# One fast-product operand, T4 of X, formed at another place: with the first pair's products instead of with the last gMLP blocks

## The chip, the core and the metric

The kernel runs on one core of a Trainium2 chip. Its engines work side by side and wait for each other through semaphores: TensorE (PE) multiplies into PSUM, VectorE (DVE) and ScalarE (ACT) do elementwise work, GpSimd (POOL) does some elementwise work and starts transfers, SyncE (SP) only starts transfers. Each engine takes its own instructions strictly in their order. The metric is device time in microseconds (us), from runs of the whole program.

## The reference

One layer of a decoder trunk on 1024 tokens of width 1024, in float32. What matters here is the input projection of the normalized tokens, `hn`, and the first mixer, gMLP:

```python
hn = rms_norm(h, norm_mix_g[l])
proj = jnp.einsum('bsd,de->bse', hn, w_in[l])
za, zb, zc, xbc, dt_raw, g_raw = jnp.split(proj, SPLIT_POINTS, axis=-1)
ya = gmlp_mixer(za, ...)    # u * (lower-triangular mix of layer_norm(v) + b), u, v = split(gelu(za))
...
gates = jax.nn.sigmoid(g_raw.reshape(bsz, seq, N_BRANCHES, D_MODEL) + b_gate[l])
merged = (gates[:, :, 0] * jnp.einsum('bse,ed->bsd', ya, w_branch_a[l])
          + gates[:, :, 1] * jnp.einsum('bse,ed->bsd', yb, w_branch_b[l])
          + gates[:, :, 2] * jnp.einsum('bse,ed->bsd', yc, w_branch_c[l]))
```

## The kernel before

**Numbers.** A float32 operand is held as two float32r parts, high and low. `split` (L129 to L133) makes them: ACT casts the high part (L132), then DVE subtracts it from the source for the low part (L133). A product is three matmuls: high by high, high by low, low by high.

**Two ways to multiply.** The columns of `proj` that need work right away are made in units of 128 columns (`product`, L555, PSUM tile `ps`). The gates, z and the Hawk gate come later, in *pairs* of 128-column blocks, by a fast scheme with seven products of half size in place of eight. Its right operands are quarters of the normalized tokens X and sums of them: B11, B21, B22, T1, T2, T3, T4. Each is four tiles of 128 x 512 in two parts. Its left operands are quarters of the pair's weights and sums of them (A.., S1 to S4). `seventh` (L478) issues the 12 matmuls of one of the seven products.

**The seven products of a pair** stand in class `Pair`, in the order in which the loop calls them:

- p1: A11 by B11 into bank b1, copied out by ACT (L983)
- p2: A12 by B21 into a bank of its own, added to p1's copy by DVE (L988)
- p4 of the pair before: A22 by T4 on top of that pair's b1
- p5: S1 by T1 into bank b2, copied out by ACT (L994)
- p6: S2 by T2 on top of b1, copied out by ACT (L1000)
- p3: S4 by B22 on top of b2, added by DVE (L1004)
- p7: S3 by T3 on top of b1, added by DVE (L1008)

A product on top of a bank has to wait until the copy of what the bank held is done: p6 waits for L983, p3 for L994, p7 for L1000. p4 of a pair runs in the next pair, so the first pair's T4 is first read after the second pair's p2.

**The place of the sums of X.** `x_forms` (L856) is a generator that makes T3, T2, T1 and T4, for two pieces kp = 0 and 1 in turn. `later` puts a generator on a list, and `step` advances each on it by one `yield`. The first gMLP unit starts it, and one step follows each later unit. A gMLP unit is `product`, a GELU (L235 to L238: two ACT and two DVE instructions) and, a step later, the mixing: 16 small matmuls (L838), two DVE instructions (L839), and on POOL the product with u (L841) and its store (L842). T3's two parts are written into tiles of X itself (L893 to L895), so this split waits until the last unit has read them. The first pair's weights are loaded and summed by `first_pair` (`cast1`, `sums1`, `sums2` at L502 to L507, `cast12`), also by steps.

**What sets the order.** In the gMLP stage a scheduler orders the instructions of each engine. In the loop over pairs, `with tc.manual_schedule()` keeps them as written: each engine has them in the order of the calls.

```python
z.w.cast22()
while z:
    nxt = Pair(*pairs.pop(0)) if pairs else None
    z.p1()
    z.w.cast34()
    step()
    z.p2()
    ...
        nxt.w.cast1()
    ...
    step()
    z.p5()
```

Of the kernel before, what the change touches and what calls it, by code (L numbers as in the profile page):

```python
# [8 lines left out]
F32 = mybir.dt.float32  # L9
# [27 lines left out]
def trunk_kernel(ctx: ExitStack, tc: tile.TileContext, x, norm_mix_g, w_in, b_gate, gmlp_ln_g, gmlp_ln_b,  # L37
# [30 lines left out]
    def nm(s):  # L68
        uid[0] += 1
        return f"{s}_{uid[0]}"  # L70

    def act(shape=(P, T), dt=F32):
        return pools[0].tile(list(shape), dt, tag="act", name=nm("a"))

    def half_(shape=(P, HF), dt=F32):
        return halfp.tile(list(shape), dt, tag="half", name=nm("h"))
# [51 lines left out]
    def split(dst_hi, dst_lo, src, eng=None, cast=None):  # L128
        if cast:  # L129
            cast.tensor_copy(out=dst_hi, in_=src)  # L130
        else:
            actv(dst_hi, src, AF.Copy)  # L132
        (eng or nc.vector).tensor_tensor(out=dst_lo, in0=src, in1=dst_hi.bitcast(F32), op=ALU.subtract)  # L133
# [62 lines left out]
    X = Pairs(lambda shape, dt_: xp.tile(list(shape), dt_, tag="xn", name=nm("xn")))  # L196
# [334 lines left out]
    queue, ready, pending = [], [], []  # L531
# [4 lines left out]
    def later(gen):  # L536
        pending.append(gen)

    def step():
        for g_ in list(pending):  # L540
            try:
                next(g_)
            except StopIteration:
                pending.remove(g_)
# [281 lines left out]
    def gmlp_unit(g):  # L826
        def stages(u2):
            if g == 0:
                later(x_forms())
            elif g == 5:  # L830
                later(first_pair())
            yield
            vg = v_of.pop(g)
            y = act()
            for half in range(2):
                ps = aux()
                for i in range(4):
                    mm(ps[:, i * P:(i + 1) * P], vg[:, half * 4 + i, :], wT[:, g, :], start=True, stop=True)  # L838
                stt(out=y[:, hsl(half)].rearrange("p (c t) -> p c t", t=P), in0=ps.rearrange("p (c t) -> p c t", t=P),  # L839
                    scalar=vh[:, LNG + g:LNG + g + 1], in1=bs[:, g, :].unsqueeze(1).to_broadcast([P, 4, P]), op0=ALU.mult, op1=ALU.add)  # L840
            nc.gpsimd.tensor_tensor(out=y, in0=y, in1=u2, op=ALU.mult)  # L841
            nc.gpsimd.dma_start(out=yd["a"][g], in_=y)  # L842

        def post(ps):
            u2 = act()
            gelu2(u2, ps, T)
            later(stages(u2))
            v_group(g + 1)

        unit_in(C_U + g * P, post)  # L850
# [2 lines left out]
    XF = {n: [[X.rhs(part, 4 * kh + kk, th) for kk in range(4)] for part in range(2)]  # L853
          for n, kh, th in (("B11", 0, 0), ("B21", 1, 0), ("B22", 1, 1), ("T3", 0, 1))}

    def x_forms():  # L856
        third = []
        for n in ("T1", "T2", "T4"):
            XF[n] = [[None] * 4, [None] * 4]
        for kp in range(2):  # L860
            def quarter(part, kh, th):
                return X.tile(part, th, 2 * kh + kp).bitcast(F32)

            def in_halves(name, t):
                for kk in range(2):
                    pr = half_((P, 4, P), F32R), half_((P, 4, P), F32R)
                    for part in range(2):
                        XF[name][part][2 * kp + kk] = pr[part]
                    split(pr[0], pr[1], t[:, kk])

            third.append(act((P, 2, 4, P)))
            t3, d, e = third[kp], act((P, 2, 4, P)), act((P, 2, 4, P))
            tt(out=t3, in0=quarter(0, 1, 1), in1=quarter(0, 0, 1), op=sub)
            tt(out=e, in0=quarter(1, 1, 1), in1=quarter(1, 0, 1), op=sub)
            tt(out=t3, in0=t3, in1=e, op=ALU.add)
            yield
            tt(out=d, in0=quarter(0, 0, 0), in1=t3, op=ALU.add)
            tt(out=d, in0=quarter(1, 0, 0), in1=d, op=ALU.add)
            in_halves("T2", d)
            yield  # L880
            tt(out=e, in0=quarter(0, 1, 1), in1=d, op=sub)
            tt(out=e, in0=quarter(1, 1, 1), in1=e, op=ALU.add)
            in_halves("T1", e)
            yield
            tt(out=d, in0=quarter(0, 1, 0), in1=d, op=sub)
            tt(out=d, in0=quarter(1, 1, 0), in1=d, op=ALU.add)
            pr = act((P, 2, 4, P), F32R), act((P, 2, 4, P), F32R)
            split(pr[0], pr[1], d)
            for part in range(2):
                for kk in range(2):  # L890
                    XF["T4"][part][2 * kp + kk] = pr[part][:, kk]
            yield
        assert not queue  # L893
        for kp in range(2):
            split(X.tile(0, 1, kp), X.tile(1, 1, kp), third[kp])  # L895

    actx_pool = []
    two = (P, 2, HF)
# [194 lines left out]
    def w_load(b, name, new, key=None):  # L1093
        L[b, key or name] = [new(two) for _ in range(2)]
        for h, t in enumerate(L[b, key or name]):
            nc.sync.dma_start(out=t, in_=w_view(b, name, h))
# [7 lines left out]
    def y_first(b, new):  # L1104
        R[b, "first"] = [new(two, F32R) for _ in range(2)]
        for h, t in enumerate(R[b, "first"]):
            nc.sync.dma_start(out=t.bitcast(F32), in_=y_view(b, "B21", h))
# [10 lines left out]
    def sums_load(b):  # L1118
        w_load(b, "A21", w4, "S")
        for h in range(2):  # L1120
            add_into(L[b, "S"][h], w_view(b, "A22", h))
# [10 lines left out]
    def make(b, i, s):  # L1132

        side, h = (s // 2) ^ (i == 3), s % 2
        new = op_new(b, i, side)
        pr = OP.setdefault((b, i), ([], []))[side]
        if side == 0:
            src = L[b, ("A12", "A11", "S", "A12", "S", "A21", "A22")[i]][h]
            hi, lo = new(two, F32R), new(two, F32R)
            split(hi, lo, src)  # L1140
            if i == 2:
                actv(src, src, AF.Copy, scale=-1.0)
                add_into(src, L[b, "A11"][h])
                for k in range(2 * h):
                    add_into(L[b, "A12"][k], L[b, "S"][k])
            elif i == 4:
                t = L[b, "A21"][h]
                tt(out=t, in0=L[b, "A11"][h], in1=t, op=sub)
        elif i == 0:
            lo = R[b, "first"][h]  # L1150
            hi = new(two, F32R)
            split(hi, lo, lo.bitcast(F32))
        else:
            hi, lo = new(two, F32R), new(two, F32R)
            split(hi, lo, R[b, ("", "B11", "B11", "B22", "B11", "B12", "B21")[i]][h])
            r = lambda name: R[b, name][h]
            if i == 1:
                tt(out=r("B11"), in0=r("B12"), in1=r("B11"), op=sub)
            elif i == 3:
                tt(out=r("B11"), in0=r("B11"), in1=r("B22"), op=sub)  # L1160
                tt(out=r("B12"), in0=r("B22"), in1=r("B12"), op=sub)
            elif i == 4:
                tt(out=r("B21"), in0=r("B21"), in1=r("B11"), op=ALU.add)
        pr.append((hi, lo))
# [113 lines left out]
    gx = ExitStack()  # L1278
    actx_pool.append(gx.enter_context(tc.tile_pool(name="actx", bufs=4, reuse_waits="tile")))
    z, prev = cur.pop(), None  # L1280
    with tc.manual_schedule():
        z.w.cast22()
        while z:
# [5 lines that stand above are left out]
            if prev:  # L1289
                step()  # L1290
                prev.p4()
            if nxt:
                nxt.w.cast1()
            else:
                w_load(0, "A12", r4)
                y_first(0, act)
                w_load(0, "A11", w4)
            step()
            z.p5()
            if nxt:  # L1300
                nxt.w.sums1()
            else:
                make(0, 0, 2)
            step()
            z.p6()
            if nxt:
                nxt.w.sums2()
                nxt.w.cast12()
            else:
                sums_load(0)  # L1310
                make(0, 0, 3)
            step()
            z.p3()
            if nxt:
                nxt.w.cast22()
            else:
                make(0, 0, 0)
            step()
            z.p7()
            if not nxt:  # L1320
                make(0, 0, 1)
            step()
            prev, z = z, nxt
# [532 lines left out]
```

## Time and profile before

| | |
|---|---|
| median of 3 runs | 1964.87 us (1964.46 to 1967.53) |
| the profiled execution's own time | 1964.1 us |
| its span, first to last instruction | 1962.4 us |
| mean granted TensorE clock | 0.991 |
| busy: PE, DVE, ACT, POOL | 97%, 72%, 52%, 13% |
| gMLP units end, first pair begins | 597.8 us, 601.3 us |

PE is busy nearly all the time, so what counts are the few places where it stands still or runs at a lower clock. The change lies between some 540 and 640 us of the span.

### The profile page before, as it was taken

How to read it: one execution, taken by the hardware profiler on the slowest of the kernel's cores; microseconds unless marked ns; L12 is line 12 of the kernel's file. 1: busy time of each engine (PE TensorE's matmuls, PEld its weight loads, DVE VectorE, ACT ScalarE, POOL GpSimd, SP SyncE). 2: the span in 40 equal slices, each digit the busy share in tenths (PEclk: the TensorE clock that was granted, in tenths of full speed). 3: DMA queues.
4: the chain of work that ended last, by engine and by line, in shares of the span. 5: the costliest groups of instructions: out<-in, count | busy, mean ns of one | idle time of the engine just before them, and what ended most of it. 6: DMA issues, size and time to landing. Idle time of an engine off the chain costs nothing.

```text
span 1962.4 us, 23743 instructions
## 1 busy us (share of the span) xinstructions
PE 1905.5 (97%) x8928; PEld 1587.2 (81%) x8928; DVE 1407.0 (72%) x2018; ACT 1014.6 (52%) x1471; POOL 262.5 (13%) x358
## 2 busy tenths in 40 slices
PE   8999999999999999999999999998999999999996
PEld 7998888888887787878778887877788887888885
DVE  5485868787758767677777888248665567787787
ACT  6425859686534545454554544167455555243253
POOL 4111122121342010100010110000211110000000
PEclk9999999999999999999999999999999999999998
DMA  4256575566754343434497987331544448553532
GB/s 162 59 147 140 119 151 122 125 154 138 166 137 153 108 150 108 150 108 129 138 286 263 275 222 199 107 108 54 198 135 170 149 169 298 168 172 118 183 118 86
DMA packets 211015, 301.25 MB, mean 154 GB/s; under 512 B 13028, under 2 KB 125876, under 8 KB 210900
## 3 DMA queue, kind: packets, MB, share of 16 engines
q1 hardware_dynamic: 167348, 158.54, 26.5%
q0 software_dynamic: 34544, 119.69, 22.8%
q10 hardware_dynamic: 9008, 21.51, 3.1%
q8 instruction: 70, 1.15, 0.3%
q14 instruction: 45, 0.37, 0.1%
HBM read 195.75 MB, written 74.58 MB: 138 GB/s over the span
## 4 chain that ended last, share of the span: by engine, by line
PE 82%; DVE 8%; ACT 5%; DMA 3%; issue 2%; POOL 0%; ACTq 0%; SPq 0%; DVEq 0%; POOLq 0%
PE aux L478 40%; PE ps L555 18%; PE gps L478 11%; PE aux L257 4%; PE aux L1378 2%; PE aux L791 1%; DMA c<-yc_d 1%; PE aux L727 1%; PE aux L723 1%; ACT a L1427 1%; PE aux L703 1%; DVE a L133 1%; DVE rsq_q L111 1%; ACT wt L132 1%; DMA a<-g_d 1%
## 5 line engine op out<-in xcount | busy, mean ns | idle before, releaser
L555 PE MATMUL ps<-xn,wh 128*128 128x512 f32 x1088 | 295.0, 392 | 0.0
L478 PE MATMUL aux<-b,b 128*128 128x512 f32 x1152 | 264.4, 389 | 1.0 <-DVE b L133 0.8
L478 PEld LDWEIGHTS aux<-b,b 128*128 128x128 f32 x1152 | 216.0, 188 | 47.0 <-DVE b L133 1.7
L555 PEld LDWEIGHTS ps<-xn,wh 128*128 128x128 f32 x1088 | 202.9, 188 | 42.2 <-issue 0.9
L478 PE MATMUL aux<-a,b 128*128 128x512 f32 x960 | 219.4, 389 | 0.0
L478 PEld LDWEIGHTS aux<-a,b 128*128 128x128 f32 x960 | 180.2, 188 | 37.4
L555 PE MATMUL ps<-xn,wl 128*128 128x512 f32 x544 | 168.3, 389 | 0.0
L478 PE MATMUL gps<-xn,wt 128*128 128x512 f32 x684 | 158.7, 389 | 2.1 <-DVE a L238 2.1
L478 PE MATMUL aux<-b,wt 128*128 128x512 f32 x672 | 156.9, 389 | 0.0
L478 PEld LDWEIGHTS gps<-xn,wt 128*128 128x128 f32 x684 | 128.2, 188 | 29.1 <-issue 2.5
L478 PEld LDWEIGHTS aux<-b,wt 128*128 128x128 f32 x672 | 126.1, 188 | 26.2
L132 ACT ACTIVATE b<-wt 128x1024 fp32r<-128x1024 f32 x88 | 90.7, 1052 | 85.4 <-DMA wt<-u_d 56.0
L133 DVE TENSOR_TENSOR wt<-a,wt 128x1024 fp32r<-128x1024 f32 x66 | 80.9, 1225 | 66.8 <-ACT wt L132 66.8
L555 PEld LDWEIGHTS ps<-xn,wl 128*128 128x128 f32 x544 | 102.1, 188 | 21.5
L133 DVE TENSOR_TENSOR b<-wt,b 128x1024 fp32r<-128x1024 f32 x88 | 107.2, 1219 | 15.5 <-ACT b L132 15.5
L1608 DVE TENSOR_TENSOR a<-aux,a 128x512 f32<-128x512 f32 x112 | 77.0, 689 | 50.4 <-PE aux L478 50.4
L133 DVE TENSOR_TENSOR a<-a,a 128x1024 fp32r<-128x1024 f32 (+1 forms) x68 | 66.6, 986 | 41.0 <-ACT a L132 40.9
L133 DVE TENSOR_TENSOR wt<-rt,wt 128x1024 fp32r<-128x1024 f32 x35 | 42.8, 1224 | 57.1 <-ACT wt L132 57.0
L132 ACT ACTIVATE a<-a 128x1024 fp32r<-128x1024 f32 (+1 forms) x68 | 55.9, 837 | 53.0 <-DVE a L1560 45.3
L478 PE MATMUL aux<-a,wt 128*128 128x512 f32 x336 | 78.7, 390 | 3.4 <-ACT a L1485 3.4
L478 PEld LDWEIGHTS aux<-a,wt 128*128 128x128 f32 x336 | 62.9, 188 | 17.2 <-ACT a L1485 4.2
L132 ACT ACTIVATE wt<-a 128x1024 fp32r<-128x1024 f32 x66 | 69.6, 1055 | 8.7 <-DVE a L506 8.3
(350 smaller groups left out, 3526.5 us busy)
## 6 DMA issues: line engine op xcount, KB each, us to landing
wt<-u_d SPq DMA_DIRECT2D x54, 512.0 KB
u_d<-a POOLq DMA_DIRECT2D x48, 512.0 KB, 5.5
raw<-in_w_in_dram SPq DMA_DIRECT2D x34, 512.0 KB
wl<-raw POOLq DMA_DIRECT2D x34, 512.0 KB, 5.2
g_d<-a POOLq DMA_DIRECT2D x24, 512.0 KB, 3.2
a<-g_d ACTq DMA_DIRECT2D x24, 512.0 KB
rt<-in_w_in_dram SPq DMA_DIRECT2D x19, 512.0 KB
a<-in_w_in_dram SPq DMA_DIRECT2D x19, 512.0 KB
```

The costliest lines, as they stand in the source:

```text
L111: stt(out=q, in0=r, scalar=nh, in1=r, op0=ALU.mult, op1=ALU.mult)
L132: actv(dst_hi, src, AF.Copy)
L133: (eng or nc.vector).tensor_tensor(out=dst_lo, in0=src, in1=dst_hi.bitcast(F32), op=ALU.subtract)
L257: mm(ps[:, :nt], X.tok(a, k, c), wk[k][w], start=(k == 0 and i == 0), stop=(k == KD - 1 and i == 2))
L478: mm(ps, lhs[l][kk], rhs[r][kk], start=(new and n == 0), stop=(n == 11), skip_group_check=not new)
L555: mm(ps[:, hsl(h)], w[wi][:, k, :], a.rhs(ai, k, h), start=(n == 0), stop=(n == 3 * KD - 1))
L703: mm(st[:, cc * 256:cc * 256 + 256], Bt[:, 2 * q + cc, :], xw[q][:, cc].rearrange("p h d -> p (h d)"), start=True, stop=True)
L723: mm(yo[:, tok(i)], pv[c // 2][:, c % 2, j * P:(j + 1) * P], Cf[:, tok(c)], start=True, stop=True)
L727: mm(yi[64 * h:64 * h + 64, tok(i)], xdt[c // 2][:, c % 2, 2 * j + h, :], E[c // 2][:, c % 2, 2 * j + h, :], start=True, stop=True)
L791: mm(ps, w[wi][:, q * P:(q + 1) * P], S["xs"][half][ai], start=(n == 0), stop=(n == 2))
L1378: mm(ps, M.tok(a, k, c), wo[nb][k][w], start=(k == 0 and a + w == 0), stop=(k == KD - 1 and a == 1))
L1608: tt(out=h, in0=ps, in1=h, op=ALU.add)
```

## The change

`x_forms` no longer makes T4. It keeps the tile that holds T2's sum (`d`, in the list `second`), from which T4 is made. A new generator, `x_last`, makes T4 for kp = 0 and then kp = 1. It is put on the list just ahead of the loop over pairs. The first pair's first `step` (behind p1 and `cast34`) so issues T4 for kp = 0, and its second `step` (behind p2 and the next pair's `cast1`) T4 for kp = 1. With one `yield` less per piece, `x_forms` gets to its other sums for kp = 1 one unit earlier, and to the split of T3 two steps earlier: that is still beside the last gMLP units.

```diff
+    third, second = [], []
+
     def x_forms():
-        third = []
         for n in ("T1", "T2", "T4"):
             XF[n] = [[None] * 4, [None] * 4]
         for kp in range(2):
...
             in_halves("T1", e)
             yield
+            second.append(d)
+        assert not queue
+        for kp in range(2):
+            split(X.tile(0, 1, kp), X.tile(1, 1, kp), third[kp])
+
+
+    def x_last():
+        for kp in range(2):
+            def quarter(part, kh, th):
+                return X.tile(part, th, 2 * kh + kp).bitcast(F32)
+
+            d = second[kp]
             tt(out=d, in0=quarter(0, 1, 0), in1=d, op=sub)
             tt(out=d, in0=quarter(1, 1, 0), in1=d, op=ALU.add)
             pr = act((P, 2, 4, P), F32R), act((P, 2, 4, P), F32R)
...
             yield
-        assert not queue
-        for kp in range(2):
-            split(X.tile(0, 1, kp), X.tile(1, 1, kp), third[kp])
...
     z, prev = cur.pop(), None
+    later(x_last())
     with tc.manual_schedule():
         z.w.cast22()
```

Three places show what it does to the order. PE, POOL and SP keep theirs. In the changed file T4's sums are L898 and L899 (before: L885 and L886), and the lines of `Pair` are ten higher (L993, L998 and L1004 are the former L983, L988 and L994).

DVE from the last unit's GELU (L236, L238) to the low part of S1 and S2 (`wt_5437`), before. `a_5234` is T4's sum for kp = 1 (L886 its second instruction), `a_5433` its low part, `h_` the halves of T1, `a_5409` and `a_5410` the weights' sums, `a_5415` a gMLP output:

```order
L236 SCALAR_TENSOR_TENSOR a_5390<-a_5390,ps_5340 128x1024
L133 TENSOR_TENSOR h_5402<-a_5235,h_5401 128x512
L886 TENSOR_TENSOR a_5234<-xn_246,a_5234 128x1024
L238 SCALAR_TENSOR_TENSOR a_5389<-a_5390,ps_5340 128x1024
L502 TENSOR_TENSOR a_5409<-a_5337 128x512
L503 TENSOR_TENSOR a_5410<-rt_5336,a_5337 128x512
L506 TENSOR_TENSOR a_5409<-a_5409,rt_5336 128x512
L839 SCALAR_TENSOR_TENSOR a_5415<-aux_5416,vh,bs 128x512
L507 TENSOR_TENSOR a_5410<-rt_5336,a_5409 128x512
L839 SCALAR_TENSOR_TENSOR a_5415<-aux_5422,vh,bs 128x512
L133 TENSOR_TENSOR a_5433<-a_5234,a_5432 128x1024
L133 TENSOR_TENSOR wt_5437<-a_5409,wt_5436 128x1024
```

The same stretch of DVE in the changed kernel; `wt_5429` is now the low part of S1 and S2:

```order
L236 SCALAR_TENSOR_TENSOR a_5394<-a_5394,ps_5344 128x1024
L238 SCALAR_TENSOR_TENSOR a_5393<-a_5394,ps_5344 128x1024
L502 TENSOR_TENSOR a_5407<-a_5341 128x512
L503 TENSOR_TENSOR a_5408<-rt_5340,a_5341 128x512
L506 TENSOR_TENSOR a_5407<-a_5407,rt_5340 128x512
L839 SCALAR_TENSOR_TENSOR a_5413<-aux_5414,vh,bs 128x512
L507 TENSOR_TENSOR a_5408<-rt_5340,a_5407 128x512
L839 SCALAR_TENSOR_TENSOR a_5413<-aux_5420,vh,bs 128x512
L133 TENSOR_TENSOR wt_5429<-a_5407,wt_5428 128x1024
```

T4's instructions and the last half of T1 are gone from among them. DVE behind this, in the changed kernel, up to the end of T4; `a_5458` is A22's low part, `wt_5481` that of S3 and S4, `wt_5505` that of the next pair's A11 and A12, and `a_4865` and `a_5149` are T4's sums:

```order
L839 SCALAR_TENSOR_TENSOR a_5432<-aux_5433,vh,bs 128x512
L839 SCALAR_TENSOR_TENSOR a_5432<-aux_5439,vh,bs 128x512
L133 TENSOR_TENSOR a_5458<-a_5341,a_5458 128x512
L133 TENSOR_TENSOR wt_5481<-a_5408,wt_5480 128x1024
L898 TENSOR_TENSOR a_4865<-xn_236,a_4865 128x1024
L899 TENSOR_TENSOR a_4865<-xn_243,a_4865 128x1024
L133 TENSOR_TENSOR a_5487<-a_4865,a_5486 128x1024
L998 TENSOR_TENSOR a_5478<-gps_5490,a_5478 128x512
L133 TENSOR_TENSOR wt_5505<-rt_5461,wt_5504 128x1024
L898 TENSOR_TENSOR a_5149<-xn_239,a_5149 128x1024
L899 TENSOR_TENSOR a_5149<-xn_246,a_5149 128x1024
L133 TENSOR_TENSOR a_5511<-a_5149,a_5510 128x1024
```

Before, the low part of T3 for kp = 1 stood among the first of these, and none of T4's six instructions. ACT over the first pair, before (L983 copies p1, L994 p5, L1000 p6):

```order
L132 ACTIVATE a_5432<-a_5234 128x1024
L132 ACTIVATE wt_5436<-a_5409 128x1024
L132 ACTIVATE a_5470<-a_5337 128x512
L983 ACTIVATE a_5490<-gps_5477 128x512
L132 ACTIVATE wt_5492<-a_5410 128x1024
L132 ACTIVATE wt_5510<-rt_5473 128x1024
L994 ACTIVATE a_5527<-aux_5514 128x512
L917 ACTIVATE a_5490<-a_5490,vh 128x512
L1000 ACTIVATE a_5527<-gps_5477 128x512
```

The same on ACT in the changed kernel:

```order
L132 ACTIVATE wt_5428<-a_5407 128x1024
L132 ACTIVATE a_5458<-a_5341 128x512
L993 ACTIVATE a_5478<-gps_5465 128x512
L132 ACTIVATE wt_5480<-a_5408 128x1024
L132 ACTIVATE a_5486<-a_4865 128x1024
L132 ACTIVATE wt_5504<-rt_5461 128x1024
L132 ACTIVATE a_5510<-a_5149 128x1024
L1004 ACTIVATE a_5527<-aux_5514 128x512
L927 ACTIVATE a_5478<-a_5478,vh 128x512
L1010 ACTIVATE a_5527<-gps_5465 128x512
```

T4's two casts (`a_5486`, `a_5510`) now stand between the copy of p1 and the copy of p5.

## Rows read from the trace of the kernel before

**Rows 1.** The page, part 1: busy time, share and instructions of each engine.

```profile
PE 1905.5 (97%) x8928; PEld 1587.2 (81%) x8928; DVE 1407.0 (72%) x2018; ACT 1014.6 (52%) x1471; POOL 262.5 (13%) x358
```

**Rows 2.** PE's waits from 570 to 660 us: total us, times, longest.

```profile
PE aux L478 <- DVE wt L133: 2.4, 1, 2.4
PE gps L478 <- DVE a L238: 2.1, 1, 2.1
```

**Rows 3.** PE's timeline around the first pair: start us, us, instruction, count, [idle before].

```profile
585.11 1.95 PE L838 MATMUL aux<-wT,a 128*128 128x128 f32 x16
...
597.79 3.73 PE L838 MATMUL aux<-wT,a 128*128 128x128 f32 x32
601.28 2.98 PE L478 MATMUL gps<-xn,wt 128*128 128x512 f32 x12
606.35 3.00 PE L478 MATMUL gps<-xn,wt 128*128 128x512 f32 x12 [2.09 <-DVE a L238]
...
612.25 4.06 PE L478 MATMUL aux<-h,wt 128*128 128x512 f32 x10 [2.36 <-DVE wt L133]
616.11 3.05 PE L478 MATMUL gps<-h,wt 128*128 128x512 f32 x12
619.00 3.08 PE L478 MATMUL aux<-xn,wt 128*128 128x512 f32 x12
621.92 8.32 PE L478 MATMUL gps<-xn,wt 128*128 128x512 f32 x36
```

**Rows 4.** DVE's timeline of the same stretch.

```profile
588.85 1.22 DVE L238 SCALAR_TENSOR_TENSOR a<-a,ps 128x1024 f32<-128x1024 f32 x1 [1.20 <-ACT a L237]
...
603.86 1.21 DVE L886 TENSOR_TENSOR a<-xn,a 128x1024 f32<-128x1024 f32 x1
605.00 1.21 DVE L238 SCALAR_TENSOR_TENSOR a<-a,ps 128x1024 f32<-128x1024 f32 x1
606.13 0.68 DVE L502 TENSOR_TENSOR a<-a 128x512 f32<-128x512 f32 x1
...
609.86 1.21 DVE L133 TENSOR_TENSOR a<-a,a 128x1024 fp32r<-128x1024 f32 x1
610.99 1.21 DVE L133 TENSOR_TENSOR wt<-a,wt 128x1024 fp32r<-128x1024 f32 x1
612.12 1.40 DVE L839 SCALAR_TENSOR_TENSOR a<-aux,vh,bs 128x512 f32<-128x512 f32 x2
613.44 2.08 DVE L133 TENSOR_TENSOR xn<-a,xn 128x1024 fp32r<-128x1024 f32 x1
615.44 2.88 DVE L133 TENSOR_TENSOR a<-a,a 128x512 fp32r<-128x512 f32 x1
...
619.39 0.68 DVE L988 TENSOR_TENSOR a<-gps,a 128x512 f32<-128x512 f32 x1
619.99 1.21 DVE L133 TENSOR_TENSOR wt<-rt,wt 128x1024 fp32r<-128x1024 f32 x1
```

**Rows 5.** ACT's timeline of the same stretch.

```profile
585.37 1.02 ACT L235 ACTIVATE a<-ps 128x1024 f32<-128x1024 f32 x1 [8.65 <-PE ps L555]
...
599.30 1.01 ACT L235 ACTIVATE a<-ps 128x1024 f32<-128x1024 f32 x1
...
605.17 1.06 ACT L132 ACTIVATE a<-a 128x1024 fp32r<-128x1024 f32 x1 [0.74 <-DVE a L886]
...
615.91 1.05 ACT L132 ACTIVATE wt<-rt 128x1024 fp32r<-128x1024 f32 x1
616.86 0.59 ACT L994 ACTIVATE a<-aux 128x512 f32<-128x512 f32 x1
```

**Rows 6.** POOL's timeline: the last two gMLP products with u.

```profile
610.02 4.42 POOL L841 TENSOR_TENSOR a<-a,a 128x1024 f32<-128x1024 f32 x1 [12.11 <-DVE a L839]
...
615.35 2.43 POOL L841 TENSOR_TENSOR a<-a,a 128x1024 f32<-128x1024 f32 x1
```

**Rows 7.** Busy time by window: engines, then PE's granted clock, DMA share, GB/s.

```profile
613.00:616.40 3.40, 3.40 (x9) 2.61 (x9) 3.40 (x3) 1.93 (x3) 3.08 (x3) 0.50 0.17 65
```

## The prediction

> **What bounds the kernel now.** PE does: it is busy 97% of the span [rows 1]. So the change is worth what it does to PE's few idle places and to its clock. I read PE's waits around the change first, then the timelines of PE, DVE and ACT there, then the clock.
>
> Between the gMLP units and the first pair PE waits twice [rows 2]: 2.1 us ahead of p2, for the last GELU's second DVE instruction, and 2.4 us inside p5, whose third matmul needs the low part of S1 and S2. The reader is to see both in PE's timeline as idle time in brackets, at 606.35 and 612.25 [rows 3]. Behind the second wait the clock is at the half level for 613.0 to 616.4 [rows 7]. p5's ten last matmuls take 612.25 to 616.11, 3.86 us, where an undisturbed product of twelve takes 2.72 (the 36 from 621.92 on take 8.32, with a tail of some 0.16) and ten would take some 2.3: the low level costs 1.5 us.
>
> Both waits are for DVE, which is full here: from 605.00 on its instructions start one behind the other without idle time [rows 4]. T4 for kp = 1 is among them: its second sum starts at 603.86, just ahead of the GELU that p2 waits for, and its low part at 609.86, just ahead of the instruction that p5 waits for.
>
> **What the change removes, step by step.** (1) The last unit's product ends as before, at 597.79, where L838 begins [rows 3]. Its GELU begins on ACT only at 599.30, because casts of T1's halves stand ahead of it [rows 5]. One unit earlier it began 0.26 us behind the product (585.11 to 585.37) and ended on DVE at 588.85 + 1.22 = 590.07, 4.70 after ACT's start. With T4 gone and T1's halves done a unit earlier, DVE and ACT are free for it: 597.79 + 0.26 + 4.70 = 602.75 in place of 606.21. The sums that move one unit earlier (T3, T2 and T1 for kp = 1) lie beside PE's units; what covers them is the time that T4's six instructions leave free there. If they run over into this GELU, all below is later by as much; I take nothing for it.
>
> p1 runs from 601.28 to 604.0, so p2 follows it without a wait: 2.1 us gained.
>
> (2) From the GELU's second instruction to the low part of S1 and S2, DVE took 605.00 to 610.99, 5.99 us, of which T4's low part is 609.86 to 610.99, 1.13 [rows 4]. Without it: 4.86. The instruction then starts at 602.75 - 1.22 + 4.86 = 606.39 and ends at 607.60. p5 begins at 606.7, and its third matmul goes at 607.65 in place of 612.25. That is 4.6 us gained, and the low clock behind it goes too: p6 begins at about 610.0 (before: 616.11) and ends at 612.7.
>
> **What it adds.** T4's two pieces now stand in the first pair, and ACT takes its instructions in order. Both casts of T4 stand ahead of the copy of p5 (L1004, before L994). p3 goes on top of the same bank and cannot start before that copy. Before, the copy was at 616.86 [rows 5], within p6, and cost p3 nothing: it began at 619.00, right behind p6 [rows 3]. Now the copy has to wait for T4's second cast, that for the second sum, and that for everything ahead of it on DVE. Starts of one DVE instruction behind the other, from [rows 4]: 1.13 for 1024 columns (609.86 to 610.99), 0.66 for an L839 (612.12 to 613.44 for two), 0.60 for 512 columns (619.39 to 619.99). A sum that reads what the one ahead of it wrote waits for its end, 1.21. A cast ends 1.16 us behind the sum that it reads (603.86 + 1.21 = 605.07, cast to 606.23 [rows 4, 5]). From 606.39 on:
>
> - low part of S1 and S2 1.13, two L839 1.32, A22's low part 0.60, low part of S3 and S4 1.13: 610.57
> - T4, kp = 0: sum 1.21, sum to its end 1.21, cast 1.16, low part 1.13: 615.28
> - p2's add 0.60, the next pair's low part 1.13: 617.01
> - T4, kp = 1: sum 1.21, sum to its end 1.21: 619.43
> - on ACT, the cast and the copy of p5, 0.10 + 0.95 (615.91 to 616.86) + 0.59 [rows 5]: 621.07, so p3 at 621.1
>
> To this comes POOL. Its last two products with u (L841) held DVE up before: a low part of 1024 columns took 2.08 in place of 1.21, one of 512 took 2.88 in place of 0.68 [rows 4], each ending just behind the POOL instruction beside it [rows 6]. That is 0.9 + 2.2 = 3.1 us. Both POOL products are released by the L839 in this list, so they fall into it again. From below nothing, if they fall where DVE waits for a cast or reads PSUM; from above each in full, 2 x 2.4 = 4.8 (the one at 615.35 took 2.43). I take 3.1, since the mix of instructions is the same: p3 at 624.2, 5.2 us later than before, after 11.5 us of idle PE.
>
> The Trainium skill, "SBUF — State Buffer", section "Who interferes with whom", says that a Vector instruction with two SBUF inputs and a GpSimd instruction that reads SBUF exclude each other, and the later one is blocked for the whole instruction. The trace agrees in the 2.88 us row. By the page alone two full blocks could come, which gives 4.8 in place of 3.1.
>
> The clock: before, 4.5 us of idle time in two pieces were followed by one stretch at half clock that cost 1.5 us [rows 7], and that cost lies ahead of p3's old start. Now the idle time ahead of p3 is longer, so I take one such stretch behind it: 1.5, between 0 (the low level falls into the idle time) and 3.0 (two stretches). p3's own 0.2 us of wait (619.00 to 621.92 is 2.92, not 2.72) goes, since the low part of S3 and S4 is long done.
>
> Behind p3 nothing new binds: p7, p1 and p2 of the second pair, the first p4 and the second p5 follow at 2.7 us each, and DVE has 13.6 us for T4's last low part, the second pair's four sums and their split, some 5 us.
>
> **Sum.** p3's start +5.2, its own wait -0.2, clock +1.5: +6.5 us. Ends: 2.1 - 0.2 + 0 = +1.9 and 6.9 - 0.2 + 3.0 = +9.7. The profiled execution took 1964.1, so 1970.6; the median of the runs shown stands 0.77 above it, so I forecast 1971.4.
>
> **Rivals.**
>
> (a) *The two waits go and nothing takes their place.* p3 is free as soon as p5's copy is out by about 612.1, that is if the last cast of T4 ended by 611.5, some 9 us ahead of the sum above. For it: the two waits in rows 2 are surely relieved, and ACT is little busy (52% [rows 1]). Against it: DVE's list, from 606.39, holds some 12 us of plain instruction time ahead of that cast, even with no hold-up. Price: p3 at 612.7, 6.3 early, less its 0.2: 1958.4. Only an instruction order other than the one shown gives this. Chance 0.05.
>
> (b) *The new wait is there, but small.* POOL's two products fall into the gaps, and the low clock level falls into the idle time: +1.9. Or some of a larger delay is made good at a later wait of PE that is not for PE's own results. Times of 1966.8 to 1968.8. For it: the list does have two casts on which DVE waits, and an add that reads PSUM. Against it: the same two POOL products cost 3.1 before, with two L839 beside them. Chance 0.12.
>
> (c) *Forecast:* +3.9 to +9.7, 1968.8 to 1974.6. Chance 0.80. Within it stands the page's rule with two full blocks: 6.9 - 0.2 + 1.5 = +8.2, 1973.1, chance 0.2.
>
> (d) *More than that:* the copy of p1 (L993), which now waits for a store of an earlier gMLP output, comes late and holds ACT, so that S3 and S4 come late as well. Every us of it is a us on the sum. Chance 0.03.
>
> **Chances and range.** About 0.2%, 3.9 us, is what a measurement of this kernel can tell from no change. Faster 0.05 is (a), no change 0.12 is (b), slower 0.83 is (c) and (d). The range leaves out (a), the lower end of (b) and the tail of (d): 1967.4 to 1974.4.
>
> **What would show it.** Right: p2 directly behind p1, and p5's third matmul within 1 us of its first. Then one idle stretch of PE of 9 to 13 us ahead of p3, ended by ACT's copy L1004, and on DVE L898, L899 and their low parts ahead of it, one or two of them stretched beside L841. After it the half clock for some 3 us, and from there all as before, later by 4 to 9 us. Wrong: p3 right behind p6; or p2 still waiting for L238, which would say that the sums moved earlier collide with the last unit's GELU; or a second wait of several us in the second pair.

## The result and the profile after

| | before | after |
|---|---|---|
| median | 1965.41 us (1964.46 to 1967.53, 4 runs) | 1974.06 us (1973.73 to 1978.12, 4 runs) |
| ratio, 95% interval | | 1.0048 (1.0036 to 1.0061) |
| the profiled execution's own time, its span | 1964.1, 1962.4 us | 1974.04, 1972.3 us |
| mean granted TensorE clock | 0.991 | 0.987 |

The changed kernel is 8.65 us slower, where 6.5 were forecast. A second set of five runs of it, in another group of runs, gave 1973.26 beside 1965.53: 7.7 us.

PE's waits from 570 to 660 us, after (columns as in [rows 2]):

```profile
PE aux L478 <- ACT a L1004: 11.9, 1, 11.9
```

One of 11.9 us stands there now, for ACT's copy of p5; of those of [rows 2] 0.15 us is left, as the next view shows. PE's timeline after, to be read against [rows 3]. (Everything up to the first pair is 0.21 us earlier in this trace than in that of before: the last L838 row begins at 597.58 and 597.79.)

```profile
601.07 5.70 PE L478 MATMUL gps<-xn,wt 128*128 128x512 f32 x24
...
607.37 2.60 PE L478 MATMUL aux<-h,wt 128*128 128x512 f32 x10 [0.15 <-DVE wt L133]
609.81 2.88 PE L478 MATMUL gps<-h,wt 128*128 128x512 f32 x12
624.55 5.37 PE L478 MATMUL aux<-xn,wt 128*128 128x512 f32 x12 [11.85 <-ACT a L1004]
629.75 8.37 PE L478 MATMUL gps<-xn,wt 128*128 128x512 f32 x36
...
640.68 2.88 PE L478 MATMUL aux<-h,wt 128*128 128x512 f32 x12
```

The 24 matmuls at 601.07 are p1 and p2 without a gap. p5 and p6 follow, done at 612.69. Then PE stands still until p3 at 624.55, and p3's twelve matmuls take 5.20 us (to 629.75) where they took 2.92 in [rows 3]. The row at 640.68 is the second pair's p5.

What p3 waited for is read on ACT:

```profile
616.42 1.06 ACT L132 ACTIVATE a<-a 128x1024 fp32r<-128x1024 f32 x1 [9.11 <-DVE a L899]
...
622.96 1.06 ACT L132 ACTIVATE a<-a 128x1024 fp32r<-128x1024 f32 x1 [4.53 <-DVE a L899]
623.92 0.58 ACT L1004 ACTIVATE a<-aux 128x512 f32<-128x512 f32 x1
```

ACT stands still for 9.11 and 4.53 us, each time with a cast of T4 at the head of its queue. p5 ended at 609.97, but its copy L1004 came only behind the second cast. Why the casts were late is read on DVE:

```profile
608.56 1.57 DVE L133 TENSOR_TENSOR a<-a,a 128x512 fp32r<-128x512 f32 x1
610.05 3.94 DVE L133 TENSOR_TENSOR wt<-a,wt 128x1024 fp32r<-128x1024 f32 x1
613.92 1.21 DVE L898 TENSOR_TENSOR a<-xn,a 128x1024 f32<-128x1024 f32 x1
...
621.64 1.23 DVE L899 TENSOR_TENSOR a<-xn,a 128x1024 f32<-128x1024 f32 x1
```

POOL beside it:

```profile
606.35 3.23 POOL L841 TENSOR_TENSOR a<-a,a 128x1024 f32<-128x1024 f32 x1 [8.57 <-DVE a L839]
610.50 2.41 POOL L841 TENSOR_TENSOR a<-a,a 128x1024 f32<-128x1024 f32 x1
```

This is the forecast's list in its order. The two low parts at its head took 1.57 and 3.94 us in place of 0.68 and 1.21: 0.89 + 2.73 = 3.6 us (3.1 were taken). Each ends about its own plain duration behind the end of one of POOL's products: 610.13 behind 609.58, and 613.99 behind 612.91. So each seems to have begun its work only when that product was through.

The clock, by windows (columns as in [rows 7]):

```profile
616.00:624.50 8.50, 0.00 (x0) 0.00 (x0) 6.09 (x7) 3.55 (x5) 0.00 (x0) 0.50 0.57 210
624.60:629.60 5.00, 5.00 (x12) 3.94 (x13) 4.46 (x6) 2.57 (x4) 0.00 (x0) 0.50 0.09 16
...
1233.80:1240.60 6.80, 6.19 (x15) 4.89 (x16) 3.08 (x4) 0.08 (x1) 0.00 (x0) 0.50 0.92 345
1390.90:1394.20 3.30, 2.82 (x7) 2.24 (x8) 3.27 (x5) 1.18 (x3) 0.00 (x0) 0.50 1.05 346
```

The clock is at its half level (1.2 GHz) in the last 8.5 us of the wait and through all of p3, and full (2.4 GHz) from p7 on: its row of 36 matmuls took 8.37 us, as before. The last two windows, far behind the change, are at the half level too.

To tell the change from such places elsewhere, I cut each profile's span into three: up to p1's start, from there to the start of the second pair's p5, and the rest. Before, that p5 is in this row of PE's timeline:

```profile
632.80 2.88 PE L478 MATMUL aux<-h,wt 128*128 128x512 f32 x12
```

so the middle piece was 632.80 - 601.28 = 31.52 us, and after 640.68 - 601.07 = 39.61: **+8.1 us**. The rest was 1962.4 - 632.80 = 1329.6 us, and after 1331.6. Of the 9.9 us between the two spans, 2.0 lie behind the second p5. Whether they belong to the change is a question for the experiments.

### The profile page after: what moved, and what is told of

It is laid out like the page before. It is cut to its first block, busy times and chain, and to the rows that moved or that the text cites. A ratio compares the mean times of both kernels' runs of the same rounds, so it can differ in the third digit from the quotient of the medians.

```text
span 1972.3 us, 23737 instructions
## 1 busy us (share of the span) xinstructions
PE 1908.0 (97%) x8928; PEld 1589.4 (81%) x8928; DVE 1411.8 (72%) x2018; ACT 1014.2 (51%) x1471; POOL 259.1 (13%) x358
## 4 chain that ended last, share of the span: by engine, by line
PE 82%; DVE 7%; ACT 5%; issue 3%; DMA 2%; POOL 1%; SPq 0%; POOLq 0%; ACTq 0%; DVEq 0%
PE aux L478 41%; PE ps L555 17%; PE gps L478 12%; PE aux L257 4%; PE aux L1389 2%; PE aux L791 1%; PE aux L727 1%; PE aux L723 1%; ACT a L1438 1%; DVE rsq_q L111 1%; PE aux L703 1%; DVE wt L133 1%; PE aux L838 1%; ACT a L132 1%; DVE a L133 0%
## 5 line engine op out<-in xcount | busy, mean ns | idle before, releaser
L133 DVE TENSOR_TENSOR a<-a,a 128x512 fp32r<-128x512 f32 (+1 forms) x68 | 65.3, 966 | 43.5 <-ACT a L132 43.5
L132 ACT ACTIVATE a<-a 128x512 fp32r<-128x512 f32 (+1 forms) x68 | 55.7, 837 | 65.6 <-DVE a L1571 45.0
```

## The experiments

Theory: PE pays for ACT's queue. T4's second cast stands ahead of p5's copy and waits for a long list on DVE, which POOL's two products make longer; the half clock comes with PE's idle time. Rivals: T4's work in the pairs costs this much wherever it stands there (DVE has no room for it); or the loss is mostly the clock's. The two marked "again" are unedited; the other kernels below are edits of the changed kernel. Lines move with the edits; the copies of p5 and p6 (L1004, L1010) and the adds of p2, p3 and p7 (L998, L1014, L1018) are named by what they are.

| kernel | median, runs | before beside it | ratio (95%) | p1 to second p5 | rest |
|---|---|---|---|---|---|
| before | 1965.41, 4 | | | 31.52 | 1329.6 |
| before again | 1964.55, 11 | 1965.53 | 0.9995 (0.9986 to 1.0004) | 31.59 | 1330.1 |
| changed | 1974.06, 4 | 1965.41 | 1.0048 (1.0036 to 1.0061) | 39.61 | 1331.6 |
| changed again | 1973.26, 5 | 1965.53 | 1.0044 (1.003 to 1.0058) | 39.10 | 1330.6 |
| T4 three steps later | 1970.53, 11 | 1965.16 | 1.0025 (1.0016 to 1.0034) | 35.48 | 1330.7 |
| sums early, casts late | 1965.08, 11 | 1965.16 | 1.0001 (0.9992 to 1.0009) | 30.72 | 1330.4 |
| second piece one step later | 1969.56, 8 | 1965.53 | 1.0024 (1.0014 to 1.0034) | 35.71 | 1329.4 |
| no products on POOL | 1969.99, 11 | 1965.16 | 1.0022 (1.0013 to 1.0031) | 35.00 | 1328.9 |
| PE kept busy | 1973.0, 5 | 1965.53 | 1.0041 (1.0029 to 1.0054) | 37.22 | 1331.6 |
| half in gMLP, half behind p7 | 1960.81, 11 | 1965.16 | 0.9978 (0.997 to 0.9987) | 26.87 | 1331.5 |

The last two columns come from one profile each, worked out as above from the rows shown with each kernel.

**T4 three steps later.** Both pieces come behind p5's copy, one behind p6 and one behind p3.

```diff
     def x_last():
+        for _ in range(3):
+            yield
         for kp in range(2):
```

> The changed kernel, with x_last started three steps later: T4's pieces are issued behind p6 and behind p3 of the first pair. On ACT both casts then stand behind the copies of p5 and p6, so p3 no longer waits. Theory (VectorE's total work between the last GELU and p4 is what binds; T4's wait only moves): p3 begins right behind p6, at about 612.5, but the add of p7 (which frees the bank for p4) stands behind T4's second piece on VectorE and comes at about 631; p4 waits for it and begins near 631.5 where it stood at 630.1 before: with a low clock behind the wait some 3 us slower than before, 1968. Rival (only ACT's order was wrong): no wait at all, 5.6 us faster than before, 1960.

Measured 1970.53. PE's timeline:

```profile
602.64 5.70 PE L478 MATMUL gps<-xn,wt 128*128 128x512 f32 x24
...
614.07 0.61 PE L478 MATMUL aux<-xn,wt 128*128 128x512 f32 x2
...
633.06 5.22 PE L478 MATMUL gps<-a,a 128*128 128x512 f32 x12 [6.72 <-DVE a L1020]
638.12 2.88 PE L478 MATMUL aux<-h,wt 128*128 128x512 f32 x12
```

p3 goes right behind p6 now (614.07), so T4's work in the pairs need not hold it up; whether its casts or its sums did is left to the next kernel. But the same work then stands ahead of p7's add (L1020 here) on DVE, and p4, which needs the bank that this add reads, waits 6.7 us and runs at the half clock (0.50 granted from 633.1 to 637.8; 5.06 us to p5's start in place of 2.72). Both were expected, p4's start to within 0.2 us from p1's. But the clock cost 2.3 us where some 1.6 were taken, and the median is 5.4 us above before, where some 3 were expected.

**Sums early, casts late.** The sums stay in the first two steps, and casts and low parts go to the fourth and fifth.

```diff
             tt(out=d, in0=quarter(1, 1, 0), in1=d, op=ALU.add)
+            yield
+        yield
+        for kp in range(2):
+            d = second[kp]
             pr = act((P, 2, 4, P), F32R), act((P, 2, 4, P), F32R)
```

> The changed kernel, with T4's sums left at the first two steps but its casts and low parts moved behind p6 and p3: VectorE has all the sums where the changed kernel has them, ACT's copy of p5 is no longer behind a cast of T4. Theory (p3 waits because the copy of p5 is queued behind T4's casts on ACT): p3 right behind p6 again, p7 begins near 618, p4 near 628.3 in place of 630.1, waiting some 2 us for the add of p7: 0 to 2 us faster than before, 1963.5 to 1965.5. Rival (VectorE's sums as such hold p3 up): p3 still near 620, as slow as the changed kernel, 1970 or more.

Measured 1965.08: the kernel before's time. PE's timeline:

```profile
603.04 5.70 PE L478 MATMUL gps<-xn,wt 128*128 128x512 f32 x24
...
614.47 0.61 PE L478 MATMUL aux<-xn,wt 128*128 128x512 f32 x2
...
620.25 8.46 PE L478 MATMUL gps<-xn,wt 128*128 128x512 f32 x36 [1.67 <-ACT a L1014]
630.92 3.00 PE L478 MATMUL gps<-a,a 128*128 128x512 f32 x12 [2.21 <-DVE a L1022]
633.76 2.88 PE L478 MATMUL aux<-h,wt 128*128 128x512 f32 x12
```

T4's second sum for kp = 1 on DVE:

```profile
621.25 1.22 DVE L899 TENSOR_TENSOR a<-xn,a 128x1024 f32<-128x1024 f32 x1
```

All four sums still stand on DVE in the steps where the change put them; the first begins at 615.89 and the last ends at 622.47. p3 begins at 614.47, right behind p6, and does not wait for them. So the two casts on ACT carried the wait over to PE. Besides 0.93 us inside p3, two small waits remain. p7 waits 1.67 us for p6's copy: this stands on ACT behind a gate (L931) that waits for p2's add, and the add stands on DVE behind the first two sums. p4 waits 2.21 us for p7's add. So the sums hold up p7 a little, and not p3. The granted clock is 1.00 from 603.0 to 634.0: it did not fall in or behind these waits.

**Second piece one step later.** Only T4 for kp = 1 moves, from behind p2 to behind p5.

```diff
             yield
+            if kp == 0:
+                yield
```

> The changed kernel, with T4 for kp = 1 one step later, behind p5 and not ahead of it; kp = 0 stays. On ACT the copy of p5 is then behind one cast of T4, the copy of p6 behind the other. Theory (each copy on ACT is late by the VectorE work that the casts ahead of it wait for): the copy of p5 comes at 618.3 and p3 starts at 618.9 (changed kernel 624.6, before 619.0), the copy of p6 at 625.1 and p7 starts at 625.8 (changed 629.8, before 621.9): two idle pieces of PE in place of one, 4 us behind the kernel before without the clock and 5 to 6 with it, 1970 to 1971. Rival (one cast ahead of the copy of p5 costs as much as two): p3 near 624, 1974.

Measured 1969.56. PE's timeline:

```profile
604.31 5.70 PE L478 MATMUL gps<-xn,wt 128*128 128x512 f32 x24
...
622.20 5.49 PE L478 MATMUL aux<-xn,wt 128*128 128x512 f32 x12 [6.29 <-ACT a L1006]
629.00 8.47 PE L478 MATMUL gps<-xn,wt 128*128 128x512 f32 x36 [1.31 <-ACT a L1012]
...
640.02 2.88 PE L478 MATMUL aux<-h,wt 128*128 128x512 f32 x12
```

The first cast alone makes p3 wait 6.3 us, and the second now stands ahead of the copy of p6 (1.3 us for p7). The wait on p3 divides between the two casts: 6.3 of 11.9 us with the first alone. From p1's start p3 begins at 17.89 and p7 at 24.69, both within 0.1 us of what was expected.

**No products on POOL.** The last two gMLP units' products with u (L841) are left out, and with them that factor of their output.

```diff
-            nc.gpsimd.tensor_tensor(out=y, in0=y, in1=u2, op=ALU.mult)
+            if g < 6:
+                nc.gpsimd.tensor_tensor(out=y, in0=y, in1=u2, op=ALU.mult)
```

> The changed kernel without GpSimd's product with u in the last two gMLP units (that part of gMLP is left out, the rest is there). Theory (the two GpSimd products hold VectorE's list up by 3.6 us in the profile of the changed kernel): p3 begins 3.6 us earlier, at 620.9, and the whole is 3 to 4 us faster than the changed kernel, 1970.5. Rival (they fall into other waits): no difference, 1974.

Measured 1969.99. The two low parts on DVE, held up before, and PE's p1, p3, p7 and second p5:

```profile
608.69 0.68 DVE L133 TENSOR_TENSOR a<-a,a 128x512 fp32r<-128x512 f32 x1
609.28 1.22 DVE L133 TENSOR_TENSOR wt<-a,wt 128x1024 fp32r<-128x1024 f32 x1
```

```profile
601.20 5.70 PE L478 MATMUL gps<-xn,wt 128*128 128x512 f32 x24
...
621.00 4.47 PE L478 MATMUL aux<-xn,wt 128*128 128x512 f32 x12 [8.22 <-ACT a L1005]
625.31 8.33 PE L478 MATMUL gps<-xn,wt 128*128 128x512 f32 x36
...
636.20 2.88 PE L478 MATMUL aux<-h,wt 128*128 128x512 f32 x12
```

From p1, p3 starts at 19.80 us in place of 23.48: 3.7 us less, about as much as the two rows lost (3.6). POOL's hold-up passes in full through DVE and ACT to PE. The remaining 8.2 us of wait are the list itself.

The Trainium skill ("SBUF — State Buffer", "Who interferes with whom") says that a Vector instruction with two SBUF inputs and a GpSimd instruction that reads SBUF take turns, and that the one which comes later is blocked until the other is through. The traces agree on the taking of turns: the row of 3.94 us ends 1.08 us behind GpSimd's product, and without that product it takes 1.22. They don't show cleanly who comes first: by the records that Vector row began at 610.05, ahead of the product at 610.50, and was still the one that was held.

**PE kept busy.** Between p6 and p3 of the first pair, 44 matmuls into a spare bank that nobody reads. The rest is as changed.

```diff
             z.p6()
+            if not prev:
+                spare = aux()
+                for n in range(44):
+                    mm(spare, z.w.op["S1"][0][n % 4], XF["T1"][0][n % 4], start=(n == 0), stop=(n == 43))
             if nxt:
```

> The changed kernel with 44 matmuls into a spare bank, which nobody reads, between p6 and p3 of the first pair: 10.0 us of work in the 11.9 us in which PE stood idle. Theory (the low clock behind the idle time is a cost of its own, 2.5 us in p3): p3 starts at the same time, 624.5, but runs at the full clock in 2.7 us and not 5.2; some 2.4 us faster than the changed kernel, 1971.6. Rival (the clock costs nothing that matters, the delay is in the wait alone): as the changed kernel, 1974.

Measured 1973.0. PE's timeline, and the clock by windows:

```profile
602.50 5.70 PE L478 MATMUL gps<-xn,wt 128*128 128x512 f32 x24
...
613.93 10.13 PE L1320 MATMUL aux<-h,wt 128*128 128x512 f32 x44
625.99 3.02 PE L478 MATMUL aux<-xn,wt 128*128 128x512 f32 x12 [1.92 <-ACT a L1004]
628.84 8.32 PE L478 MATMUL gps<-xn,wt 128*128 128x512 f32 x36
...
639.72 2.88 PE L478 MATMUL aux<-h,wt 128*128 128x512 f32 x12
```

```profile
625.90:628.80 2.90, 2.81 (x12) 2.35 (x13) 2.87 (x5) 1.32 (x4) 0.00 (x0) 1.00 0.03 6
```

p3 starts 23.49 us behind p1, as in the changed kernel, but at the full clock: 2.85 us in place of 5.20 and (changed again) 4.72. So the idle time ahead of p3 is what its half clock comes from, and it costs 1.9 to 2.4 us there. The whole kernel's time does not show the gain: 1973.0 beside 1973.26 of five runs each, which scatter over 4 us. In these two profiles the 1.9 us gained in the middle piece are met by 1.25 us more ahead of p1 (602.50 and 601.25) and 1.0 in the rest, which the edit does not touch. So the runs do not show what the clock is worth to the whole.

**Changed again and before again**, both unedited, ran beside "second piece one step later" and "PE kept busy".

> The changed kernel itself, for a second profile and more times. The first profile's other low clock stretches, near 1233.8 (twice as long as before) and 1390.8 (none before there), add 2 us to it behind the change. Theory (they lie where PE waits for something else and differ from execution to execution, not by the change): in this profile they stand at other places or in another number, and the delay built up by the second pair is 7.5 to 8.5 us again. Rival (they come of the change): the same places and the same 2 us again.

> The kernel before itself, for a second profile. Theory (low clock stretches in the merge and the up projection differ from execution to execution): they stand at other places, or in another number, than in the first profile, and the time lies between 1963 and 1968 as before. Rival (they belong to the program): low stretches at 1227, 1313 and 1357 again and none near 1384.

Measured 1973.26 and 1964.55. PE's timeline of the changed kernel's second profile, and its clock at the first of the two late places:

```profile
601.25 5.70 PE L478 MATMUL gps<-xn,wt 128*128 128x512 f32 x24
...
624.73 4.89 PE L478 MATMUL aux<-xn,wt 128*128 128x512 f32 x12 [11.88 <-ACT a L1004]
629.45 8.35 PE L478 MATMUL gps<-xn,wt 128*128 128x512 f32 x36
...
640.35 2.88 PE L478 MATMUL aux<-h,wt 128*128 128x512 f32 x12
```

```profile
1233.00:1239.70 6.70, 5.87 (x14) 4.62 (x15) 3.29 (x4) 0.29 (x1) 0.00 (x0) 0.50 0.94 349
```

The wait is the same to 0.03 us, and the middle piece is 39.10. At 1390 the clock is full this time (1.00 from 1390.0 to 1394.0): that low place belongs to an execution, not to the kernel. The one at 1233 is there in both profiles of the changed kernel. Before, the same place was at half clock too, for about half as long (1.00 again from 1230.8 to 1234.2):

```profile
1227.40:1230.70 3.30, 3.30 (x9) 2.61 (x8) 0.80 (x3) 0.61 (x1) 0.00 (x0) 0.50 0.77 259
```

The second profile of the kernel before has this place again at the same length (0.50 from 1227.4 to 1230.7), as well as those near 1313 and 1357 (0.50 and 0.51), and none near 1384 (1.00 from 1383 to 1389). That is what the rival of its expectation said, and not its theory: these places came again in the same program, and of the late places named here only that at 1390 was a matter of one execution. In the first pair this profile differs from the first one:

```profile
601.00 2.98 PE L478 MATMUL gps<-xn,wt 128*128 128x512 f32 x12
606.08 4.58 PE L478 MATMUL gps<-xn,wt 128*128 128x512 f32 x12 [2.10 <-DVE a L238]
...
632.59 2.88 PE L478 MATMUL aux<-h,wt 128*128 128x512 f32 x12
```

The first wait is there again, but the half clock lies on p2 (0.50 from 606.1 to 609.4), and in place of the 2.4 us inside p5 stand waits of 0.86 us in p5, 0.32 ahead of p6 and 0.93 in p3. The length from p1 to the second p5 is nevertheless the same, 31.59 beside 31.52 us.

The rest of the span is 1329.6 and 1330.1 us before, 1331.6 and 1330.6 changed, and 1328.9 to 1331.6 in the other kernels, with no order in which it follows the edit: the low place near 1230 lasts some 7 us, as changed, in "PE kept busy" and "half in gMLP, half behind p7", some 3.5 us, as before, in "T4 three steps later" and "sums early, casts late", and is missing in the other two. Two profiles of each kernel don't decide whether the change adds about 1 us there.

**Half in gMLP, half behind p7.** T4 for kp = 0 goes back to the gMLP units, in the step of T1's sum; T4 for kp = 1 comes behind p7, where p2's, p3's and p7's adds stand ahead of it on DVE. `t4(d, kp)` is the body of `x_last`'s loop.

```diff
             in_halves("T1", e)
+            if kp == 0:
+                t4(d, kp)
             yield
...
     def x_last():
...
+        for _ in range(5):
             yield
+        t4(second[1], 1)
```

> T4 for kp = 0 is made in the gMLP stage, in the same step as T1 for kp = 0, T4 for kp = 1 behind p7 of the first pair, after the adds of p3 and p7. Theory (VectorE has room for one piece near 550 us and for one between p7 and p4, but not between the last GELU and p3): both waits of the kernel before go and none takes their place; p3 near 612.5, p7 near 616.3, p4 near 624.5 in place of 630.1: 5 to 6 us faster than before, 1960, which beats both kernels. Rival (the piece put into gMLP delays the last GELU, or p4 waits for the late piece): no faster than before.

Measured 1960.81 (1958.41 to 1963.77): faster than both kernels, and 4.35 us below the 1965.16 beside it, where 5 to 6 us were expected. PE's timeline:

```profile
601.55 5.70 PE L478 MATMUL gps<-xn,wt 128*128 128x512 f32 x24
...
614.52 2.56 PE L478 MATMUL aux<-xn,wt 128*128 128x512 f32 x10 [0.90 <-DVE wt L133]
...
627.15 1.43 PE L478 MATMUL gps<-a,a 128*128 128x512 f32 x5 [0.32 <-DVE a L133]
628.42 2.88 PE L478 MATMUL aux<-h,wt 128*128 128x512 f32 x12
```

The gMLP stage has room for one piece of T4, and the first pair for the other, if it comes behind the copies and adds that free banks. Both waits of [rows 2] are gone, 0.90 + 0.32 us of others are left, and the granted clock is 1.00 from 601.6 to 628.4.

## Why the forecast came out as it did

The mechanism was right: the waits that went, the one that came and what made it. What failed is the size of two terms of the sum. The first is the clock's, "one such stretch behind it: 1.5": p3 grew by 2.3 and 1.8 us in the two profiles, where 1.3 was forecast (1.5 less 0.2 for its own wait). The second is POOL's hold-up, 3.6 us where 3.1 was taken. The sum was too small by 1.0 to 1.6 us in the middle piece. Times are those of each trace; where two traces are compared, they are taken from p1's start.

- **The waits removed.** p2 stands directly behind p1, as forecast. The last GELU's second DVE instruction ends at 602.46 (602.75 forecast, and this trace is 0.21 early). p5's third matmul waits 0.15 us. p6 ends at 612.69 (612.7).
- **The wait added.** p3 starts 23.48 us behind p1, before 17.72 (619.00 - 601.28): +5.8 where 5.2 were forecast. The plain list was right: the second T4 sum for kp = 1 was to end at 619.43 without POOL, and 619.43 + 3.6 = 623.0 stands beside the measured 621.64 + 1.23 + 0.21 = 623.1. What was off is POOL's hold-up, 3.6 and not 3.1. The row of 512 columns lost 0.89 and the one of 1024 columns 2.73; I had carried over a loss of 2.2 and one of 0.9 from [rows 4].
- **The clock.** This is the step that was sized worst: "one such stretch behind it: 1.5, between 0 and 3.0". p3's twelve matmuls took 5.20 and 4.72 us, against 2.92 before, so +2.3 and +1.8 where -0.2 + 1.5 = +1.3 was forecast. I priced the half clock by [rows 7], where it covered ten matmuls for part of their time; here it covered all or most of p3, 5.0 us in the first profile and not "some 3". The price was low even for [rows 7]: 3.86 less 2.27 is 1.6, and p6 behind it took 2.89 in place of 2.72, 1.8 together. With PE kept busy the cost is gone from p3.
- **"Behind p3 nothing new binds."** It held: PE waits for nothing else up to 660 us.
- **Sum.** Middle piece +8.1 and +7.5 in the two profiles, forecast +6.5. The medians' +8.65 and +7.7 lie close to these; the first may hold up to 1 us from the half clock further on, which stays open. Of the 2.7 us by which the time forecast, 1971.4, fell short of 1974.06, 0.5 is the kernel before, whose median went from 1964.87 to 1965.41 with a fourth run. The range given, to 1974.4, also cuts 0.2 us off the forecast's own case (c), to 1974.6, which its text does not say.
- **Rivals.** (a) did not come: p3 is not free after p5's copy could have been made, since the order on ACT decides. With the casts late p3 does come right behind p6, but other waits take the place (1.67 and 2.21 us), and the time was 1965.08, not 1958.4. (b) did not come: no product of POOL fell into a gap. Two full blocks, 4.8 us, did not come either: the first product (to 609.58) was more than half through when the row that it held up began (608.56), and cost 0.89. The 1973.1 given for two blocks lies close to 1974.06 and 1973.26, but by luck: its 4.8 for POOL was too much and its 1.5 for the clock too little. (d) did not come: L993 ran at 605.79, in time.

## What to carry to other kernels

Before moving work into another stretch, walk the in-order queue of each engine that it touches and ask which instruction behind it frees something: here two casts on ACT that waited for DVE stood ahead of a copy that frees a PSUM bank, and cost PE 11.9 us, while the sums themselves cost p3 nothing. Put such work behind the copies and adds that free banks, and divide it between two stretches that each have room for a part (1960.81 us), rather than move it whole from a full one to another; both pieces behind p7 were not tried. Price an idle stretch of PE with what the clock takes from the product behind it: against 2.72 us it took 1.6 to 2.6 here behind idle stretches of 6.3 to 11.9 us. Compare traces piece by piece, because the pieces that the edit does not touch differ by up to some 3 us from one profile to another (p1 begins between 601.07 and 604.31 in kernels that are alike up to there).

## What was not expected

- The half clock of p3 began in the idle time and went on through the product: 8.5 us of the wait at 0.50, then 5.0 us of work at 0.50.
- Where the clock falls can change with the execution: behind p2's or p5's wait in the two profiles of the kernel before, at 1390 in one of the two of the changed kernel, while the other late places came again. And the kernel before ran 1962.73 to 1968.12 us in 33 runs beside one group, though nothing in it differed. A few us of a kernel like this can't be read from a few runs.
